# Attention in a hybrid decoder trunk: the transposed P moves from the three rotating score banks to the two banks of the value products

## The chip, the cores and the metric

The kernel runs on one core of one Trainium2 chip. The metric is the device time of one execution in microseconds, as the median of three runs. Engines are named as in the profile: PE (TensorE matmul), PEld (its weight loads), DVE (VectorE), ACT (ScalarE), POOL (GpSimd), SP (the queue that issues the DMAs). PSUM, into which PE writes, has eight banks of 128 partitions by 512 fp32 values. PE, ACT, DVE and POOL each work through a fixed list of instructions in order: an instruction that waits holds up all that stand behind it on the same engine.

## The reference

Two layers; each normalises x, multiplies it by one wide input matrix, runs two groups of heads side by side (a gated linear recurrence, HGRN2, and a sliding-window attention), gates both with SiLU, multiplies by an output matrix and adds the normalised result to x. SEQ is 512, D_MODEL 1024, and there are 16 attention heads of 64 in 2 key groups, with a window of 128. What matters here is the attention:

```
s = einsum('bnqkgd,bnskd->bnkgqs', qb, kw) * ATT_SCALE      # 128 queries x 256 keys per block
s = where(mask, s, NEG_INF)                                  # causal, at most 127 back
p = softmax(concatenate([s, sink], -1), -1)[..., :-1]        # one learned sink per head
o = einsum('bnkgqs,bnskd->bnqkgd', p, vw)
h_layer:  proj = h @ w_in;  y = concat(o_h, o_a) @ w_out;  x = x + rms_norm(y, g_post)
```

## The kernel before

**Projections.** All large products are done in three passes of split fp32 (`mm3`, L174 to L177): a value is held as a rounded part "hi" and a remainder "lo", and lo·hi, hi·lo and hi·hi are added in one PSUM bank. The weights come in pieces of 128x512 by DMA (`raw`); ACT rounds each to `whi` (L169), and DVE (for some POOL) subtracts it to get `wlo` (L170). The projection products write the three banks `pj`. They make up most of PE's work, and they are what fills PE while other stages wait for ACT, DVE and POOL.

**Banks.** Of the eight banks, three are `pj`, three rotate under `sc()` (each call takes the next of `sc0` to `sc2`, strictly in turn), and two are a pool under `ac()` (a call takes whichever is free):

```
sc_tiles = [ps.tile([P, 512], F32, tag=f"sc{i}", name=f"sc{i}", bufs=1) for i in range(SC)]
def sc():
    sc_turn[0] += 1
    return sc_tiles[sc_turn[0] % SC]
def ac():
    return ps.tile([P, 512], F32, tag="ac", name="ac", bufs=8 - PJ - SC)
```

**Attention.** Per layer there are 16 steps i = 4g + n, for four groups g of four heads and four blocks n of 128 queries. Each step has three parts, called here S, T and U:

- S(i), `att_scores`: the scores of four heads. For n = 0 they fill one bank (L417, eight matmuls of 128x128). For the other n they fill two banks, the halves S(i)a and S(i)b, of two heads each (L428, four matmuls of 128x256 per half). DVE masks them in place (L420, L432), takes the row maxima (L421, L433) and makes the bias `negm` (L436) and `ds` (L438); ACT takes the exponentials, one per head (L442, a READ_ACCUMULATOR row behind each), and `es` (L445); DVE adds and inverts the sums (L446, L447); POOL multiplies P by them (L449). The exponentials are the last readers of a score bank.
- T(i), `att_transpose`: PE transposes the four heads' P into one bank (L455); ACT rounds it (L267, out `a`), DVE takes the remainder (L268), and these two free the bank. POOL cuts out the two triangles `pcur` (or `b`) and `pprev` (L467).
- U(i), `att_value`: the value product in an `ac` bank (L481, four matmuls, two for n = 0). ACT copies one half out (`u`, L483), DVE adds the other to it in two instructions (`oa`, L487); the second of these frees the bank.

`att_stream` writes S(i), T(i-2), U(i-4) in turn, and `merge` weaves these 50 parts evenly into the projection steps that remain up to the first forget/query slab, FQ. A scheduler then fixes each engine's order: it keeps the written priority, but holds an instruction back while, by its own estimate, its bank or its inputs are not free. So who owns a bank decides where S, T and U stand among the projection matmuls. After the attention comes the recurrence (`hgrn`), which draws on both `sc` and `ac`. While the last attention steps run, ACT also works off FQ (L526 to L529: a load of its function table, two sigmoids, two scalings).

Of the kernel before, what the change touches and what calls it, by code (L numbers as in the profile page):

```python
# [65 lines left out]
def hybrid_kernel(ctx: ExitStack, tc: tile.TileContext, x, wkv, win, wout, g_pre, g_post, lbp, ghead, sinks,  # L66
# [12 lines left out]
    def pin(ins):  # L79
        return tc.keep_in_program_order(ins)  # L80
# [7 lines left out]
# [7 lines that stand above are left out]
    def tmp(tag, dt=F32, n=1):  # L95

        t = tp.tile([P, n, 512] if n > 1 else [P, 512], dt, tag=tag, name=tag, bufs=TB[tag])
        return t
# [167 lines left out]
    def split_psum(hi, lo, src):  # L266
        nc.scalar.copy(hi, src)  # L267
        nc.vector.tensor_tensor(lo, src, hi.bitcast(F32), op=ALU.subtract)  # L268
# [55 lines left out]
    def layer(l, last):  # L324
# [125 lines left out]
            return pt  # L450

        def att_transpose(g, n, pt, odd):
            T = sc()
            for h in range(4):
                pin(nc.tensor.transpose(T[:, h * P:(h + 1) * P], pt[:, h * P:(h + 1) * P], ident))  # L455
            tt_ = tmp("a", F32R, 2)
            split_psum(tt_[:, 0], tt_[:, 1], T)
            if n == 0:
                return [(n, tt_[:, 0]), (n, tt_[:, 1])]
            terms = []  # L460
            for which in range(2):
                if which == 0:
                    d = big.tile([P, 2, 512], F32R, tag="oy", name="pcur", bufs=6) if odd else tmp("b", F32R, 2)
                else:
                    d = big.tile([P, 2, 512], F32R, tag="q", name="pprev", bufs=QB)
                sg = -1 if which == 0 else 1
                nc.gpsimd.affine_select(out=d.rearrange("p a (h t) -> p (a h) t", h=4),  # L467
                                        in_=tt_.bitcast(F32).rearrange("p a (h t) -> p (a h) t", h=4),
                                        pattern=[[0, 8], [-sg, P]], compare_op=ALU.is_ge, fill=0.0,
                                        base=-which, channel_multiplier=sg)  # L470
                terms += [(n - which, d[:, 0]), (n - which, d[:, 1])]
            return terms
# [16 lines left out]
        def att_stream(steps):  # L489
            pts, terms = {}, {}  # L490
            n = len(steps)
            for tt in range(NT):
                ensure(("k", l, tt))
            for i in range(n + VLAG):
                if i < n:
                    until(lambda: steps[i][0] in qs)
                    pts[i] = att_scores(*steps[i])
                    yield 1.0
                if 2 <= i <= n + 1:
                    terms[i - 2] = att_transpose(*steps[i - 2], pts.pop(i - 2), i % 2)  # L500
                    yield 1.0
                if i >= VLAG:
                    att_value(*steps[i - VLAG], terms.pop(i - VLAG))
                    yield 1.0
# [181 lines left out]
        def zh_stream(s):  # L686
            def evac(tt, o):
# [9 lines left out]
                def rest():  # L697
                    T = sc()
                    for j in range(4):
                        pin(nc.tensor.transpose(T[:, j * P:(j + 1) * P], g[:, j * P:(j + 1) * P], ident))  # L700
                    Tv = T.rearrange("p (j t) -> p j t", j=4)
                    nc.scalar.activation(hi[:, :, t_], Tv, AF.Copy, scale=gh[:, l:l + 1])
                    nc.vector.scalar_tensor_tensor(lo[:, :, t_], Tv, gh[:, l:l + 1], hi[:, :, t_].bitcast(F32), op0=ALU.mult, op1=ALU.subtract)
# [153 lines left out]
def _tables():  # L857
# [3 lines left out]
    c, s = np.cos(ang).astype(np.float32), np.sin(ang).astype(np.float32)  # L861
    cf = np.ascontiguousarray(np.tile(c.T, (4, 1)))
    sf = np.ascontiguousarray(np.tile(s.T, (4, 1)))
# [47 lines left out]
```

## Time and profile before

| | |
|---|---|
| median of 3 runs | 956.77 us (952.09 to 960.68) |
| the profiled execution | 954.91 us, span 953.2 us, mean granted TensorE clock 0.989 |
| PE, PEld busy | 918.9 us (96%), 754.8 us (79%) |
| DVE, ACT, POOL busy | 681.9 us (72%), 475.2 us (50%), 267.3 us (28%) |
| attention on PE | about 80 to 188 us (layer 0) and 548 to 658 us (layer 1) |

The span runs from the first to the last instruction. Times in the traces count from its start. In a row of the timeline stand start, duration, engine, source line, what is written from what, and in brackets the idle time of the engine ahead of it with what ended it. Matmuls are pipelined, so that the duration of one (0.39 us) is longer than the distance to the next (0.23 us), which is what counts on PE. In a table of windows each row is a stretch of the span, with the busy time and the instructions of each engine, and the granted TensorE clock (PEclk, 1.00 is full).

### The profile page before, as it was taken

What the parts mean: (1) busy time and instruction counts of PE and PEld (TensorE: products, weight loads), DVE (VectorE), ACT (ScalarE), POOL (GpSimd) and SP (SyncE); (2) the same over time, 40 slices, a digit from 0 to 9 for tenths busy, and PEclk for the clock granted to TensorE, in tenths of its full rate; (3) what the DMA queues carried; (4) which work ended last, traced back from release to release, by engine and by line L of the source; (5) the groups of instructions that cost most, each with busy time, mean ns of one, the idle gap of its engine ahead of it and who ended that gap; (6) DMA issues with size and microseconds to landing.
All of it is one profiled execution on the core that took longest, in us unless ns stands there. A gap on an engine that the chain in (4) does not pass through costs nothing.

```text
span 953.2 us, 19110 instructions
## 1 busy us (share of the span) xinstructions
PE 918.9 (96%) x7228; PEld 754.8 (79%) x7228; DVE 681.9 (72%) x1382; ACT 475.2 (50%) x1135; POOL 267.3 (28%) x282
## 2 busy tenths in 40 slices
PE   7999998999999999999969989989999999999996
PEld 5887887778878788788868878877788887887885
DVE  5866878796766685865795678778867578749546
ACT  5524766836464462434553257677363645414242
POOL 2232454422231221311331235434322213113102
PEclk8999999999999999999999999999999999999999
DMA  6456622232222332323443665122222233413313
GB/s 219 145 177 175 186 72 79 66 90 68 78 79 81 87 112 89 112 69 118 132 158 123 178 180 150 54 70 67 90 67 69 88 89 84 129 55 103 89 46 132
DMA packets 56716, 101.34 MB, mean 106 GB/s; under 512 B 6448, under 2 KB 8880, under 8 KB 56624
## 3 DMA queue, kind: packets, MB, share of 16 engines
q1 hardware_dynamic: 56624, 100.12, 35.5%
q8 instruction: 57, 0.93, 0.4%
q14 instruction: 35, 0.29, 0.1%
HBM read 87.52 MB, written 12.58 MB: 105 GB/s over the span
## 4 chain that ended last, share of the span: by engine, by line
PE 77%; DVE 9%; ACT 6%; issue 4%; POOL 2%; DMA 1%; SPq 0%; DVEq 0%; POOLq 0%; ACTq 0%
PE pj L175 22%; PE pj L177 21%; PE pj L176 21%; DVE wlo L170 3%; ACT s L442 2%; PE sc L583 2%; PE sc L428 2%; PE ac L652 1%; PE ac L481 1%; PE ac L640 1%; ACT whi L169 1%; PE ac L655 1%; DVE xn L306 1%; PE sc L455 1%; PE sc L700 1%
## 5 line engine op out<-in xcount | busy, mean ns | idle before, releaser
L169 ACT CAST whi<-raw 128x512 fp32r<-128x512 f32 x256 | 158.2, 620 | 193.5 <-PE pj L177 154.3
L170 DVE TENSOR_TENSOR wlo<-raw,whi 128x512 fp32r<-128x512 f32 x248 | 185.4, 753 | 63.0 <-ACT whi L169 61.0
L175 PE MATMUL pj<-hhi,wlo 128*128 128x512 f32 x512 | 206.4, 403 | 0.0
L177 PE MATMUL pj<-hhi,whi 128*128 128x512 f32 x512 | 200.8, 392 | 0.0
L176 PE MATMUL pj<-hlo,whi 128*128 128x512 f32 x512 | 200.2, 391 | 0.0
L177 PEld LDWEIGHTS pj<-hhi,whi 128*128 128x128 f32 x512 | 96.6, 189 | 21.0
L175 PEld LDWEIGHTS pj<-hhi,wlo 128*128 128x128 f32 x512 | 96.6, 189 | 18.7
L176 PEld LDWEIGHTS pj<-hlo,whi 128*128 128x128 f32 x512 | 96.8, 189 | 18.2
L175 PE MATMUL pj<-whi,hlo 128*128 128x512 f32 x256 | 103.2, 405 | 3.6 <-ACT whi L169 3.6
L175 PE MATMUL pj<-whi,ops 128*128 128x512 f32 x256 | 103.8, 406 | 0.0
L176 PE MATMUL pj<-wlo,hhi 128*128 128x512 f32 x256 | 100.4, 392 | 0.0
L177 PE MATMUL pj<-whi,ops 128*128 128x512 f32 x256 | 100.1, 391 | 0.0
L177 PE MATMUL pj<-whi,hhi 128*128 128x512 f32 x256 | 100.1, 391 | 0.0
L176 PE MATMUL pj<-wlo,ops 128*128 128x512 f32 x256 | 99.7, 390 | 0.0
L601 POOL TENSOR_TENSOR k<-k,tot 128x256 f32<-128x256 f32 x80 | 65.0, 832 | 109.9 <-PE sc L583 64.0
L175 PEld LDWEIGHTS pj<-whi,hlo 128*128 128x128 f32 x256 | 48.2, 188 | 12.6 <-ACT whi L169 4.5
L449 POOL TENSOR_TENSOR s<-s,sums 128x512 f32<-128x512 f32 x32 | 34.9, 1091 | 81.9 <-DVE sums L447 34.3
L177 PEld LDWEIGHTS pj<-whi,ops 128*128 128x128 f32 x256 | 48.0, 188 | 10.7
L600 DVE TENSOR_TENSOR q<-q,tot 128x256 f32<-128x256 f32 x80 | 46.9, 614 | 13.1 <-PE sc L583 8.6
L177 PEld LDWEIGHTS pj<-whi,hhi 128*128 128x128 f32 x256 | 48.1, 188 | 10.1
L175 PEld LDWEIGHTS pj<-whi,ops 128*128 128x128 f32 x256 | 48.1, 188 | 9.3
L176 PEld LDWEIGHTS pj<-wlo,ops 128*128 128x128 f32 x256 | 48.2, 188 | 9.0
(172 smaller groups left out, 1587.0 us busy)
## 6 DMA issues: line engine op xcount, KB each, us to landing
raw<-in_win_dram SPq DMA_DIRECT2D x192, 256.0 KB, 2.7
raw<-in_wout_dram SPq DMA_DIRECT2D x64, 256.0 KB, 2.7
stack<-rot SPq DMA_DIRECT2D x16, 512.0 KB, 3.9
qs<-stack SPq DMA_DIRECT2D x32, 256.0 KB, 4.4
a<-in_x_dram SPq DMA_DIRECT2D x12, 256.0 KB, 3.1
raw<-in_wkv_dram SPq DMA_DIRECT2D x8, 256.0 KB, 4.0
x_mid<-a SPq DMA_DIRECT2D x8, 256.0 KB, 2.1
a<-x_mid SPq DMA_DIRECT2D x8, 256.0 KB, 3.2
```

Source lines behind the costliest of these rows:

```text
L169: nc.scalar.copy(hi, v)
L170: (nc.gpsimd if i in on_pool and i % 2 else nc.vector).tensor_tensor(lo, v, hi.bitcast(F32), op=ALU.subtract)
L175: nc.tensor.matmul(o, lhsT=sta[1], rhs=mov[0], start=start, stop=False)
L176: nc.tensor.matmul(o, lhsT=sta[0], rhs=mov[1], start=False, stop=False)
L177: nc.tensor.matmul(o, lhsT=sta[0], rhs=mov[0], start=False, stop=stop)
L306: nc.vector.scalar_tensor_tensor(xn, xt[c], r, g[c], op0=ALU.mult, op1=ALU.mult)
L428: pin(nc.tensor.matmul(S[:, h * 256:(h + 1) * 256], lhsT=q[:, 2 * hp_ + h, t_], rhs=kst[v][p][:, (n - 1) * P:(n + 1) * P], start=(h == 0 a ...
L442: nc.scalar.activation(pt[:, h * P:(h + 1) * P], cur[h], AF.Exp, bias=negm[:, h:h + 1], scale=SCALE, accum_out=sums[:, h:h + 1])
L449: nc.gpsimd.tensor_tensor(pv, pv, sums.unsqueeze(2).broadcast_to([P, 4, P]), op=ALU.mult)
L583: pin(nc.tensor.matmul(L[32 * b:32 * b + 32, c:c + 16], lhsT=k[:, o_:o_ + 32], rhs=qv[:, blk:blk + qu, 1, :], start=True, stop=True, tile_ ...
L600: nc.vector.tensor_tensor(qv[:, :, 1, :], qv[:, :, 1, :], tv[:, :, 0].unsqueeze(2).broadcast_to([P, nb, hh]), op=ALU.mult)
L601: nc.gpsimd.tensor_tensor(kv_[:, :, 0, :], kv_[:, :, 0, :], tv[:, :, 1].unsqueeze(2).broadcast_to([P, nb, hh]), op=ALU.mult)
```

## The change

T takes its bank from `ac()` instead of `sc()`. The scores have the three `sc` banks to themselves during the attention, and T and U share the two `ac` banks. Nothing is computed differently, and no instruction is added or removed.

```diff
         def att_transpose(g, n, pt, odd):
-            T = sc()
+            T = ac()
             for h in range(4):
                 pin(nc.tensor.transpose(T[:, h * P:(h + 1) * P], pt[:, h * P:(h + 1) * P], ident))
             tt_ = tmp("a", F32R, 2)
             split_psum(tt_[:, 0], tt_[:, 1], T)
```

What the change moves is the order on the engines. The places below are from layer 0; layer 1 has the same changes at nearly the same places. `sc_78` to `sc_80` are the three rotating score banks, x4 is a run of four equal rows.

PE at the head of the attention, from shortly behind S(1) to T(0). Before:

```order
L176 MATMUL pj<-wlo,hhi 128x512
L175 MATMUL pj<-whi,hlo 128x512
L177 MATMUL pj<-whi,hhi 128x512
L175 MATMUL pj<-whi,hlo 128x512 x2
L176 MATMUL pj<-wlo,hhi 128x512
L177 MATMUL pj<-whi,hhi 128x512
L428 MATMUL sc_79<-kst,qs 128x256 x4
L428 MATMUL sc_80<-kst,qs 128x256 x4
L175 MATMUL pj<-whi,hlo 128x512
L176 MATMUL pj<-wlo,hhi 128x512
L177 MATMUL pj<-whi,hhi 128x512
L455 MATMUL sc_78<-ident,s 128x128 x4
```

and now, the same stretch up to the two halves of S(2):

```order
L176 MATMUL pj<-wlo,hhi 128x512
L428 MATMUL sc_78<-kst,qs 128x256 x4
L177 MATMUL pj<-whi,hhi 128x512
L175 MATMUL pj<-whi,hlo 128x512
L176 MATMUL pj<-wlo,hhi 128x512
L177 MATMUL pj<-whi,hhi 128x512
L175 MATMUL pj<-whi,hlo 128x512 x2
L176 MATMUL pj<-wlo,hhi 128x512 x2
L177 MATMUL pj<-whi,hhi 128x512
L428 MATMUL sc_79<-kst,qs 128x256 x4
L428 MATMUL sc_80<-kst,qs 128x256 x4
```

A half of S(3), in sc_78, now stands ahead of S(2), 14 projection matmuls behind S(1); its bank was that of S(1)b. T(0) and T(1) then follow S(2) as one run of eight, and T(2) stands right behind S(4), ten projection matmuls earlier than before.

PE in the middle, around S(14), group 3, block 2. Before:

```order
L177 MATMUL pj<-hhi,whi 128x512
L175 MATMUL pj<-hhi,wlo 128x512
L428 MATMUL sc_79<-kst,qs 128x256 x4
L176 MATMUL pj<-hlo,whi 128x512
L428 MATMUL sc_80<-kst,qs 128x256 x4
L177 MATMUL pj<-hhi,whi 128x512
```

and now:

```order
L177 MATMUL pj<-hhi,whi 128x512
L428 MATMUL sc_79<-kst,qs 128x256 x4
L428 MATMUL sc_80<-kst,qs 128x256 x4
L175 MATMUL pj<-hhi,wlo 128x512
L176 MATMUL pj<-hlo,whi 128x512
L177 MATMUL pj<-hhi,whi 128x512
```

Before, S(13) stood in the same two banks as S(14); now S(13) stands in sc_80 and sc_78, so that only the second half of S(14) meets a bank of S(13). DVE's list from S(9) to `negm` of S(13) is the same in both but for the banks' names.

PE at the tail, from T(13) to U(11). Before there are six projection matmuls between the two:

```order
L455 MATMUL sc_78<-ident,s 128x128 x4
L175 MATMUL pj<-hhi,wlo 128x512
L176 MATMUL pj<-hlo,whi 128x512
L177 MATMUL pj<-hhi,whi 128x512
L175 MATMUL pj<-hhi,wlo 128x512
L176 MATMUL pj<-hlo,whi 128x512
L177 MATMUL pj<-hhi,whi 128x512
L481 MATMUL ac<-pcur,vst 128x512 x2
L481 MATMUL ac<-pprev,vst 128x512 x2
```

and now there are eleven (T(13) and the first of them are left out here):

```order
L176 MATMUL pj<-hlo,whi 128x512
L177 MATMUL pj<-hhi,whi 128x512
L175 MATMUL pj<-hhi,wlo 128x512
L176 MATMUL pj<-hlo,whi 128x512
L177 MATMUL pj<-hhi,whi 128x512
L175 MATMUL pj<-hhi,wlo 128x512
L176 MATMUL pj<-hlo,whi 128x512
L177 MATMUL pj<-hhi,whi 128x512
L175 MATMUL pj<-hhi,wlo 128x512
L176 MATMUL pj<-hlo,whi 128x512
L481 MATMUL ac<-pcur,vst 128x512 x2
L481 MATMUL ac<-pprev,vst 128x512 x2
```

U(11) stands five projection matmuls later. Behind it, counted from U(11), T(14) now stands 10 and U(12) 17 projection matmuls on (before 7 and 12), T(15) 23, U(13) and U(14) together 32, and U(15) 36 (before 18, 21, 47 and 50).

## The prediction

> **What bounds the kernel now.** I read the page first, then the waits of PE in each layer's attention, then windows around the places where PE stops, and last the timelines there.
>
> ```profile
> PE 918.9 (96%) x7228; PEld 754.8 (79%) x7228; DVE 681.9 (72%) x1382; ACT 475.2 (50%) x1135; POOL 267.3 (28%) x282
> ...
> PE 77%; DVE 9%; ACT 6%; issue 4%; POOL 2%; DMA 1%; SPq 0%; DVEq 0%; POOLq 0%; ACTq 0%
> ```
>
> PE is busy for 918.9 of the span's 953.2 us, and holds 77% of the chain that ended last: only PE's idle time can be won or lost. Next are PE's waits from 78 to 190 us (attention of layer 0; in total, times, longest), and the first two of the same list from 548 to 660 us (layer 1).
>
> ```profile
> PE sc L428 <- ACT s L442: 2.9, 2, 2.5
> PE pj L175 <- ACT whi L169: 1.4, 1, 1.4
> PE ac L481 <- DVE oa L487: 0.2, 1, 0.2
> PE sc L455 <- ACT es L445: 0.2, 1, 0.2
> PE sc L417 <- ACT s L442: 0.2, 1, 0.2
> PE sc L455 <- issue: 0.2, 1, 0.2
> PE sc L455 <- DVE negm L436: 0.2, 1, 0.2
> ```
>
> ```profile
> PE sc L428 <- ACT s L442: 2.9, 2, 2.6
> PE pj L175 <- ACT whi L169: 2.2, 1, 2.2
> ...
> ```
>
> Two waits are large: scores for exponentials (2.9 us in each layer, of which one is 2.5 or 2.6 and the other 0.4 or 0.3), and a projection product for a converted weight (1.4 and 2.2). The five short ones of layer 0 sum to 1.0 us; I take 0.9 per layer. The windows show what the large ones leave behind (the third number from the right is PEclk).
>
> ```profile
> 87.00:91.00 4.00, 2.59 (x13) 1.82 (x12) 2.30 (x8) 3.15 (x12) 2.60 (x2) 1.00 0.00 1
> 155.00:158.00 3.00, 1.08 (x5) 0.56 (x3) 2.97 (x6) 0.86 (x3) 1.75 (x2) 1.00 0.59 170
> 158.00:161.00 3.00, 2.37 (x10) 2.27 (x11) 2.54 (x7) 1.37 (x9) 0.77 (x1) 0.52 0.21 72
> 161.00:164.00 3.00, 3.00 (x16) 2.48 (x16) 1.74 (x6) 1.18 (x5) 1.04 (x1) 0.91 0.00 0
> 556.00:560.00 4.00, 1.78 (x8) 1.18 (x7) 1.93 (x6) 3.76 (x17) 2.25 (x2) 1.00 0.00 0
> 628.00:631.00 3.00, 2.93 (x13) 2.60 (x14) 2.89 (x10) 0.81 (x6) 1.07 (x2) 0.69 0.17 61
> 631.00:634.00 3.00, 3.00 (x13) 2.44 (x13) 1.04 (x3) 1.63 (x8) 0.17 (x1) 0.74 0.01 3
> 700.00:800.00 100.00, 100.00 (x1065) 82.17 (x1064) 70.52 (x131) 48.13 (x94) 23.18 (x29) 1.00 0.27 80
> ```
>
> In the recurrence (700 to 800) PE has no gap, and by the order of the instructions none of its matmuls there changes its place. So the whole effect must come from the two attention stages. There PE stops at the head of each layer (87 to 91, 556 to 560) and in the middle (155 to 158 in layer 0, ahead of 628 in layer 1). Behind the middle stop the clock falls: it costs 3 x (0.48 + 0.09) = 1.7 us in layer 0 and 3 x (0.31 + 0.26) = 1.7 us in layer 1. At the head it stays at 1.00.
>
> **The middle stop.** Rows of PE, POOL, DVE and ACT in order of time, layer 0.
>
> ```profile
> 155.47 0.39 PE L177 MATMUL pj<-hhi,whi 128*128 128x512 f32 x1
> 155.70 0.39 PE L175 MATMUL pj<-hhi,wlo 128*128 128x512 f32 x1
> ...
> 156.25 1.48 POOL L467 TENSOR_SCALAR_AFFINE_SELECT pcur<-a 128x1024 fp32r<-128x1024 f32 x1 [3.15 <-DVE a L268]
> 156.70 1.04 DVE L436 SCALAR_TENSOR_TENSOR negm<-mx,nsnk 128x4 f32<-128x4 f32 x1
> ...
> 158.38 0.20 ACT L442 ACTIVATION_READ_ACCUMULATOR s<-sc,negm 128x1 f32 x1
> ...
> 158.63 1.22 PE L428 MATMUL sc<-kst,qs 128*128 128x256 f32 x4 [2.55 <-ACT s L442]
> ```
>
> S(14)a, at 158.63, waited 2.55 us for a bank of S(13), until the second exponential of S(13) was read at 158.58. Those exponentials waited for `negm`, which took 1.04 us on DVE beside POOL's `pcur`. Is the bank the cause? Only in part. Now S(14)a has a free bank, but S(14)b stands right behind it in the bank of S(13)a, and needs the same two exponentials. DVE's list up to that `negm` is unchanged and the T and U ahead keep their places, so the exponentials end when they did. PE does half a score during the stop, in place of one projection matmul: 0.48 us (S(1), quoted below: eight matmuls in 1.12 us less a tail of 0.16, halved) less 0.23 (155.70 - 155.47), at half clock twice that. **-0.5 us per layer.** The stop shrinks from 2.55 to about 2.3 us. I take the clock to fall as before; if it does not, 1.7 us per layer go too.
>
> The other wait of L428 is S(13)b for S(12), 0.37 us. S(12) and S(13) now stand in three different banks: **-0.4 us per layer**. The short waits all stand at places that change: **-0.9**, and what is new is counted below.
>
> [...]
>
> **The head.** Here the change costs. The scheduler sees a free bank earlier, and puts half of S(3) 14 projection matmuls behind S(1), in the bank of S(1)b.
>
> ```profile
> 82.24 1.12 PE L428 MATMUL sc<-kst,qs 128*128 128x256 f32 x8
> ...
> 88.47 0.21 ACT L442 ACTIVATION_READ_ACCUMULATOR s<-sc,negm 128x1 f32 x1
> ...
> 89.34 0.50 PE L175 MATMUL pj<-whi,hlo 128*128 128x512 f32 x1 [1.41 <-ACT whi L169]
> ...
> 96.50 1.04 POOL L449 TENSOR_TENSOR s<-s,sums 128x512 f32<-128x512 f32 x1 [5.59 <-DVE sums L447]
> ...
> 557.89 0.23 ACT L442 ACTIVATION_READ_ACCUMULATOR s<-sc,negm 128x1 f32 x1
> ...
> 558.77 0.50 PE L175 MATMUL pj<-whi,hlo 128*128 128x512 f32 x1 [2.22 <-ACT whi L169]
> ```
>
> S(1) gives way to the projections at 83.20; 14 matmuls of 0.23 us later it is 86.4. The bank is free when the fourth exponential of S(1) has been read, at 88.68. So PE stops there for 2.2 us ahead of work that it could do: before, it issued six more projection matmuls and then waited 1.41 us for `whi`. At 89.3 it is six matmuls (1.4 us) behind and half a score (0.5) ahead, and `whi` is there by then. Layer 0: **+0.9 us**. In layer 1 the half stands 17 matmuls behind S(1), three ahead of the old stop; it is released at 558.1 and ends at 558.6, while the old stop ended at 558.77: 0.7 - 0.5 - 0.1 = **+0.1 us**.
>
> T(2) comes ten matmuls earlier, right behind S(4). Before, POOL's product for step 2 ended at 97.54. S(2) came six matmuls behind 89.34 and ended at 91.9, so that the way from S(2) to T(2) takes 5.6 us. Now 12 projection matmuls, T(0), T(1), half a score and S(4) lie between: 2.8 + 0.9 + 0.5 + 1.0 = 5.2 us (a T is about half of S(1)'s eight matmuls). It is 0.4 us too early, and 1.4 if the maxima of S(3)a and the cast of T(1), which stand ahead of step 2 now, add their 0.4 and 0.6: 0 to 1.4 us; I take 0.8, since both stand there in the order. **+0.8 us per layer.**
>
> **The tail.** T and U now pass through two banks: U(11) waits for the bank of U(10), T(14) for that of T(13), U(12) for that of U(11). Rows of PE, ACT and DVE, layer 0:
>
> ```profile
> 169.72 0.62 PE L481 MATMUL ac<-pcur,vst 128*128 128x512 f32 x2
> 169.76 0.58 ACT L483 COPY u<-ac 64x512 f32<-64x512 f32 x1
> ...
> 170.38 0.85 DVE L487 TENSOR_TENSOR oa<-ac,u 64x256 f32<-64x256 f32 x2 [1.54 <-ACT u L483]
> ...
> 173.14 0.60 ACT L267 CAST a<-sc 128x512 fp32r<-128x512 f32 x1
> ...
> 173.77 0.69 DVE L268 TENSOR_TENSOR a<-sc,a 128x512 fp32r<-128x512 f32 x1
> 174.38 1.05 DVE L170 TENSOR_TENSOR wlo<-raw,whi 128x512 fp32r<-128x512 f32 x1
> ...
> 175.69 1.24 DVE L170 TENSOR_TENSOR wlo<-raw,whi 128x512 fp32r<-128x512 f32 x1
> ```
>
> U(10)'s bank is free at 171.23, when both `oa` are done; its copy stood on ACT behind FQ until 169.76. U(11) was issued at 169.72; five matmuls later is 170.9: a wait of 0.4 us. T(14) needs the remainder of T(13), done at 174.46; PE is there at 171.3 + 0.9 + 10 x 0.23 = 174.5: none. U(12) needs the two `oa` of U(11). U(11)'s copy stands on ACT behind the cast of 173.14 and two weight casts and ends near 175.5; DVE has the remainder and two `wlo` ahead until 176.7 (174.38, 175.69; both beside POOL), and 0.85 us of `oa` make 177.6. PE comes at 174.5 + 0.4 + 7 x 0.23 = 176.5: a wait of 1.1 us. T(15), U(13), U(14) and U(15) have 4 to 15 matmuls of room each, and by the same count find their banks free. **+1.5 us per layer**; from nothing, with `wlo` at its undisturbed 0.69 us (that of L268) and ACT early, to 3, with one more 1.24 us ahead of U(12) or U(13). In the steady steps T and U have most of a step to empty a bank, and wait for nothing.
>
> Also moved: in layer 1, SP issues a store of rotated queries ahead of a weight piece that had to wait for its buffer. The store goes earlier, the piece does not: nothing.
>
> **Sum.** Layer 0: -0.5 - 0.4 - 0.9 + 0.9 + 0.8 + 1.5 = +1.4; layer 1: +0.6 (the head 0.8 less). Together **+2.0 us**. On the profiled execution (954.91, which is 1.86 us under the median) this is 956.9, on the median of 956.77 it is 958.8; I give 957.8, between them. The waits move from bank to bank; the chain of DVE, ACT and POOL in a step is as long as it was.
>
> **Rivals.**
> 1. *The score waits go.* DVE gets its masks earlier, `negm` slips ahead of POOL's `pcur`, and both middle stops vanish with the cold clock: 2.55 + 2.6 + 3.4 = 8.5 us in place of the 1.0 counted: 957.8 - 7.5 = 950.3 us. If the new waits of T(2) and the tail were nil as well (1.6 + 3.0), 945.7. For it: this is the largest wait on the list. Against: S(14)b meets a bank of S(13), and DVE's list is the same.
> 2. *The two shared banks become the bound at the tail.* A U waits for the copy of the U before, which stands on ACT behind FQ's table load and four activations; T waits for U, and U for T. From a wait of about 2.5 us on, the clock falls as at 158: per layer 3.0 in place of 1.5, and 1.7 cold, 6.4 us in all; with the same drop behind both stops at the head another 3.4: 964 to 968 us. For it: U(10) was copied 5 us after its matmuls. Against: my count leaves waits near 1 us. [...]
> 3. *The shortened middle stops no longer drop the clock* (2.3 us, near the 2.22 that did not): 957.8 - 3.4 = 954.4 us.
>
> **How the numbers follow.** Forecast 0.62, rival 1 0.12, rival 2 0.12, rival 3 0.14. The unknown costs give from 957.8 - 1.6 - 3.0 - 3.4 = 949.8 (new waits nil, clock up) to 964 (rival 2 without the head); I let go of the outermost and take 951 to 964. About 1%, 9.6 us, is what a measurement of this kernel can tell from no change. Faster by that needs rival 1 with nothing new waiting: 0.05. Slower needs rival 2 at its upper end: 0.08. Within: 0.87.
>
> **What would show it.** In the profile after: in layer 0, L428 waiting for L442 about 2.2 us near 86.5; no wait ahead of S(13)b; S(14)b still waiting near 158, a stop of some 2.3 us with a clock near 0.5 behind it; a wait of T(2) for POOL; waits of L481 for DVE `oa` near U(11) and U(12), 1.5 us per layer; the recurrence as it was. I am wrong if the middle stop is gone, or if any tail wait exceeds 2 us.

## The result and the profile after

The change made the kernel slower: 965.43 us in the median of 9 runs (963.35 to 966.25) against 956.78 us for the kernel before (952.09 to 960.68), a ratio of 1.008 with a 95% interval of 1.006 to 1.010. That is 8.7 us where 2.0 had been forecast, and outside the range. The profiled execution took 966.25 us, the longest of the nine, so that it shows rather more than the median loses.

The page of the kernel after, its busy times and its chain:

```profile
PE 920.6 (95%) x7228; PEld 758.1 (79%) x7228; DVE 691.5 (72%) x1382; ACT 474.3 (49%) x1135; POOL 269.3 (28%) x282
...
PE 70%; DVE 13%; ACT 8%; issue 5%; POOL 3%; DMA 2%; SPq 0%; DVEq 0%; POOLq 0%; ACTq 0%
```

PE's busy time is nearly the same. What has grown is the part of the chain that is not PE: DVE went from 9% to 13%, ACT from 6% to 8%, DMA from 1% to 2%. The place is the attention, as forecast. From the start of S(0) (79.95 before, 80.76 after) to the first matmul of the recurrence (199.60 and 206.03) layer 0 took 119.7 us before and 125.3 after; layer 1 took 120.6 and 125.5. Between the two stages lie 349.0 and 349.1 us.

PE's waits after, 78 to 190 us and 548 to 670 us (in total, times, longest):

```profile
PE sc L428 <- ACT s L442: 5.0, 2, 2.9
PE ac L481 <- DVE oa L487: 2.0, 3, 0.9
PE ac L455 <- POOL s L449: 1.3, 1, 1.3
PE ac L455 <- DVE a L268: 1.3, 1, 1.3
```

```profile
PE sc L428 <- ACT s L442: 5.1, 2, 2.8
PE ac L481 <- DVE oa L487: 2.4, 4, 0.9
PE ac L455 <- POOL s L449: 1.6, 1, 1.6
PE ac L455 <- DVE a L268: 1.3, 1, 1.3
```

The same waits in their places, PE's timeline of layer 0, in order S(3)a, T(2), U(4), T(7), U(9), S(14)b, U(12), U(15):

```profile
89.53 0.79 PE L428 MATMUL sc<-kst,qs 128*128 128x256 f32 x4 [2.15 <-ACT s L442]
...
101.35 0.66 PE L455 MATMUL ac<-ident,s 128*128 128x128 f32 x4 [1.33 <-POOL s L449]
...
127.16 0.70 PE L481 MATMUL ac<-a,vst 128*128 128x512 f32 x2 [0.29 <-DVE oa L487]
...
132.82 0.63 PE L455 MATMUL ac<-ident,s 128*128 128x128 f32 x4 [1.27 <-DVE a L268]
...
158.88 0.70 PE L481 MATMUL ac<-pcur,vst 128*128 128x512 f32 x2 [0.82 <-DVE oa L487]
...
164.74 0.89 PE L428 MATMUL sc<-kst,qs 128*128 128x256 f32 x4 [2.86 <-ACT s L442]
...
183.31 0.69 PE L481 MATMUL ac<-a,vst 128*128 128x512 f32 x2 [0.90 <-DVE oa L487]
...
191.08 0.70 PE L481 MATMUL ac<-pcur,vst 128*128 128x512 f32 x2 [0.47 <-DVE oa L487]
```

Behind the stops at the head the clock fell this time (windows, third number from the right):

```profile
88.00:92.00 4.00, 2.48 (x9) 2.09 (x10) 2.06 (x7) 3.11 (x12) 2.08 (x2) 0.76 0.00 0
92.00:96.00 4.00, 4.00 (x23) 3.40 (x22) 2.46 (x7) 0.40 (x1) 0.00 (x0) 0.82 0.71 250
564.00:568.00 4.00, 3.33 (x10) 2.85 (x11) 2.41 (x6) 2.25 (x8) 1.87 (x2) 0.57 0.03 6
```

That is 4 x (0.24 + 0.18) = 1.7 us in each layer of this execution. Over the nine executions the mean granted clock was 0.982 to 0.989, so the clock did not cost the same in all of them.

Three waits were not forecast at all: U(4), T(7) and U(9), 2.4 us together. T(7) waits for a remainder on DVE. The chain of the kernel after, 118 to 128 us (start, us, what; rows of `issue` are left out), says where DVE was:

```profile
118.83 0.70 DVE wlo L170
...
119.55 4.28 DMA raw<-in_win_dram
...
123.85 0.63 ACT whi L169
...
124.51 0.69 DVE wlo L170
125.20 0.97 DVE negm L436
...
126.20 1.50 ACT s L442 x8
```

The chain goes through a **transfer of a weight piece**. `negm` of S(7) stands on DVE behind the `wlo` of that piece, and the piece had not landed. It was late because of the head. Rows of DVE and SP after, and behind them the same two and `negm` of S(7) before:

```profile
105.73 1.46 DVE L170 TENSOR_TENSOR wlo<-raw,whi 128x512 fp32r<-128x512 f32 x1
...
107.22 0.35 SPq L152 DMA_DIRECT2D raw<-in_win_dram  x1
```

```profile
99.79 0.69 DVE L170 TENSOR_TENSOR wlo<-raw,whi 128x512 fp32r<-128x512 f32 x1 [0.44 <-ACT whi L169]
...
100.51 0.35 SPq L152 DMA_DIRECT2D raw<-in_win_dram  x1
...
119.29 0.14 DVE L436 SCALAR_TENSOR_TENSOR negm<-mx,nsnk 128x4 f32<-128x4 f32 x1
```

Counted from S(0), the first `wlo` behind the masks of S(2) came after 19.8 us before and after 25.0 us now, and with it the refill of its buffer, 5.9 us later (20.6 and 26.5): a `raw` buffer, of which there are three, is filled again only when its `wlo` is done. From that first `wlo` to `negm` of S(7) DVE has eight pieces in both kernels. That `negm` ended 39.5 us after S(0) before and 45.4 us after it now, again 5.9 us later. The exponentials of S(7) and S(8) follow from it, and behind them on ACT stands the cast of T(6) (131.36), whose remainder T(7) waits for.

The transfer in this chain was also slow by itself: 4.28 us from issue to landing, where the one issued 1.2 us ahead of it took 2.61. Four loads of `qs` (256 KB each) were issued 0.4 to 1.9 us behind it. Before, the piece in the same place in SP's order had 1.6 us to the first of these loads and took 2.68 us. That the loads slow it is likely by these rows, but no run tests it.

### The profile page after: what moved, and what is told of

Read it like the earlier page. It is cut to its first block, busy times and chain, and to the rows that moved or that the text cites. A ratio compares the mean times of both kernels' runs of the same rounds, so it can differ in the third digit from the quotient of the medians.

```text
span 964.5 us, 19096 instructions
## 1 busy us (share of the span) xinstructions
PE 920.6 (95%) x7228; PEld 758.1 (79%) x7228; DVE 691.5 (72%) x1382; ACT 474.3 (49%) x1135; POOL 269.3 (28%) x282
## 4 chain that ended last, share of the span: by engine, by line
PE 70%; DVE 13%; ACT 8%; issue 5%; POOL 3%; DMA 2%; SPq 0%; DVEq 0%; POOLq 0%; ACTq 0%
PE pj L175 21%; PE pj L177 20%; PE pj L176 19%; DVE wlo L170 3%; ACT s L442 3%; PE sc L583 2%; PE ac L652 1%; PE ac L640 1%; DVE oa L487 1%; PE ac L655 1%; ACT whi L169 1%; DVE mx L433 1%; DVE a L268 1%; DVE xn L306 1%; DVE negm L436 1%
## 5 line engine op out<-in xcount | busy, mean ns | idle before, releaser
L442 ACT ACTIVATE s<-sc,negm 128x128 f32<-128x128 f32 x128 | 45.5, 368 | 43.2 <-DVE negm L436 43.1
L177 PEld LDWEIGHTS pj<-whi,hhi 128*128 128x128 f32 x256 | 48.7, 190 | 10.5
L176 PEld LDWEIGHTS pj<-wlo,hhi 128*128 128x128 f32 x256 | 48.9, 191 | 8.3
```

Source lines behind the costliest of these rows:

```text
L176: nc.tensor.matmul(o, lhsT=sta[0], rhs=mov[1], start=False, stop=False)
L177: nc.tensor.matmul(o, lhsT=sta[0], rhs=mov[0], start=False, stop=stop)
L442: nc.scalar.activation(pt[:, h * P:(h + 1) * P], cur[h], AF.Exp, bias=negm[:, h:h + 1], scale=SCALE, accum_out=sums[:, h:h + 1])
```

## The experiments

All were timed in 3 or 5 rounds beside the kernel before. The head means T(0) to T(2) and what the scheduler puts around them; the tail means T(13) on.

| kernel | median, us | ratio to before (95%) |
|---|---|---|
| the change | 965.4 | 1.008 (1.006 to 1.010) |
| T(0) to T(2) in `ac` alone | 968.5 | 1.013 (1.011 to 1.016) |
| T(3) to T(15) in `ac` alone | 956.7 | 1.001 (0.999 to 1.003) |
| T(13) to T(15) in `ac` alone | 960.4 | 1.003 (1.001 to 1.005) |
| all T in `ac`, S in the banks of before | 968.4 | 1.013 (1.010 to 1.015) |
| T(0) in `ac` alone | 963.4 | 1.006 (1.004 to 1.008) |
| T(2) to T(15) in `ac` | 959.3 | 1.002 (1.001 to 1.004) |
| the change, one turn skipped at T(0) | 962.2 | 1.005 (1.003 to 1.007) |
| four `raw` buffers, before | 954.2 | 0.997 (0.996 to 0.999) |
| four `raw` buffers, the change | 958.2 | 1.001 (1.000 to 1.003) |
| four `raw` buffers, the change, tail in `sc` | 958.0 | 1.001 (1.000 to 1.003) |
| `negm` early, before | 958.8 | 1.002 (1.001 to 1.004) |
| four `raw` buffers and `negm` early, before | 955.1 | 0.998 (0.997 to 1.000) |
| `negm` early, T(0) to T(2) in `ac` | 958.0 | 1.000 (0.998 to 1.002) |
| `negm` early, the change | 958.1 | 1.002 (1.000 to 1.003) |

### Which part of the attention costs

The line of the change was made to depend on the step:

```diff
-            T = ac()
+            T = ac() if 4 * g + n < 3 else sc()
```

> T(0), T(1) and T(2) alone take an `ac` bank, T(3) to T(15) an `sc` bank as before. By the order of the instructions half of S(3) again stands 14 projection matmuls behind S(1), and everything from S(6) on stands as in the kernel before. Theory A (the head costs: a stop of 2.2 us with a clock that falls behind it, and an early T(2)): L428 waits 2.2 us near 89 us, the clock in 88 to 92 is near 0.76, T(2) waits 1.3 us; that is +0.75 + 1.7 + 1.3 = 3.8 us in layer 0 and 0.1 + 1.7 + 1.6 = 3.4 us in layer 1, so about 964 us where the kernel before has 956.8. Theory B (T and U sharing two banks costs, in the steady steps and at the tail; the head is made up for by later slack): 957 to 958 us.

```diff
-            T = ac()
+            T = sc() if 4 * g + n < 3 else ac()
```

> The converse: T(0) to T(2) take an `sc` bank as before, T(3) to T(15) an `ac` bank as in the change, so that the head is as before and the middle and the tail are as changed. Theory A: the waits of T(7), U(4), U(9) and of the tail sum to at most 3.7 us per layer against 0.9 to 1.3 us of short waits and the wait of S(13)b that go: 960 to 962 us. Theory B: the time of the change less little, 964 to 965 us. If the whole loss is the cold clock at the head: 957 to 958 us.

```diff
-            T = ac()
+            T = ac() if 4 * g + n >= 13 else sc()
```

> T(13), T(14) and T(15) alone take an `ac` bank; the head and the steady steps are as before, and the tail stands as in the change or a little later. By the tail's rows in the change (U(12) 0.9 us, U(15) 0.4 to 0.5 us) it costs 1.4 us per layer: 959 to 960 us under both theories. 962 us or more would mean that the tail costs more than its waits show; 956 to 957 us that its waits are made up for behind it.

The three bank choices of the head alone gave 968.5 us, more than the whole change; all the others without them gave 956.7. So the loss lies at the head, as theory A has it, but it is larger than A's 7 us. The tail alone cost 3.5 us where about 3 had been expected, but that is luck: in its trace no U of the tail waits for `oa`, and the only new wait there is U(15) for POOL's `pcur` and `pprev`, 0.9 us in each layer. Nor do the parts add: the tail costs 3.5 us alone, and nothing where T(3) to T(12) are in `ac` too. PE's waits with T(3) to T(15) in `ac`, 78 to 190 us:

```profile
PE sc L428 <- ACT s L442: 2.9, 1, 2.9
PE ac L481 <- DVE oa L487: 2.1, 3, 0.9
PE pj L175 <- ACT whi L169: 1.4, 1, 1.4
```

U(9), U(12) and U(15) still wait (2.1 us together), but T(7) does not, though T and U share the two banks from T(3) on and stand from S(7) on as in the change. The sharing alone therefore does not make T(7) wait; the head has to be there too. With the head alone it has become a larger one. Its rows of PE, ACT and DVE:

```profile
123.43 0.62 ACT L169 CAST whi<-raw 128x512 fp32r<-128x512 f32 x1 [2.47 <-DMA raw<-in_win_dram]
124.08 0.69 DVE L170 TENSOR_TENSOR wlo<-raw,whi 128x512 fp32r<-128x512 f32 x1 [2.40 <-ACT whi L169]
124.69 0.16 DVE L436 SCALAR_TENSOR_TENSOR negm<-mx,nsnk 128x4 f32<-128x4 f32 x1
125.74 1.68 PE L417 MATMUL sc<-kst,qs 128*128 128x128 f32 x8 [3.44 <-ACT s L442]
```

S(8) stops for 3.44 us here (3.47 in layer 1), because its bank is one of S(7) again, whose exponentials wait for the late `negm`. Behind the stop in layer 0 PE's projection matmuls stood 0.43 us apart in place of 0.23, until about 129.6. In the change the scores have three banks to themselves, S(8) finds a free one, and T(7) waits 1.27 us: the rest of the change seems to soften what its head does.

### Which part of the head costs

```diff
+            sc()
             T = ac()
```

> T takes an `ac` bank as in the change, but one turn of the score banks is skipped at each T, so that every S stands in the bank in which it stood before: T and U share two banks and the scores gain nothing. By the order no half of S(3) stands early. Theory B (the sharing costs): T(7), U(4), U(9), U(12) and U(15) wait as in the change, 3.7 us per layer, and the middle stop of S(14) is that of before: about +5 to +7 us, 962 to 964 us. Theory A (the head costs, through the freed score banks): the clock at the head stays at 1.00, and the time is 957 to 960 us.

This missed: 968.4 us without an early half of S(3). T(7) did not wait, nor did U(4) or U(9), so theory B, which had the time too low as well, is not borne out. PE's stops were 0.48 us at T(2), 1.58 at the second half of S(5), 1.14 at T(4) and 1.29 at a half of S(9): T stands as early as `ac` allows, ahead of POOL's product, and the scores stop for banks that are not free. An early half of S(3) is thus not needed for a loss of this size; but here T and U share two banks in every step while the scores gain none, so this run alone does not say which of the two costs.

```diff
-            T = ac()
+            T = ac() if 4 * g + n == 0 else sc()
```

> T(0) alone takes an `ac` bank. By the order half of S(3) stands early, in the bank of S(1)b, as in the change, but T(1) and T(2) stand 15 and 10 projection matmuls apart behind T(0) and S(3) (350 and 360 counted from the start of the stage's list, before 345 and 354, in the change 335 and 344). Theory A1 (the early half itself costs: PE stops 2.2 us, the clock falls, and S(2) and all weight work on DVE behind it come 2 us later, which returns as later stops): 962 to 966 us. Theory A2 (T(1) and T(2), put too early, cost): only the stop and the clock are left, about 2.4 us in layer 0 and 1.8 us in layer 1: 960 to 961 us at most, and 957 to 958 us if that is made up for behind it.

```diff
-            T = ac()
+            T = sc() if 4 * g + n < 2 else ac()
```

> T(0) and T(1) take an `sc` bank as before, T(2) and all later ones an `ac` bank; the kernel with T(0) to T(2) in `sc` banks gave 956.7 us. By the order T(2) and U(0) stand five projection matmuls earlier than before, ahead of S(4) and S(5), and no half of S(3) stands early. Theory A1 (only the early half costs): 956 to 958 us. Theory A2 (an early T is enough): T(2) waits 1 to 1.5 us for POOL's product, the steps behind it come late, 960 to 966 us.

```diff
+            if 4 * g + n == 0: sc()
             T = ac()
```

> As the change, with one turn of the score banks skipped ahead of T(0): S(3) stands in the banks in which it stood before. By the order its first two matmuls stand 22 projection matmuls behind S(1) and no longer 14, where their bank is about free, and T(0), T(1) and T(2) stand as early as in the change (336 and 342). Theory A1: the stop at the head is under 0.5 us, the clock stays at 1.00, and the time is 957 to 960 us. Theory A2: T(2) waits 1.3 us or more, and 962 to 967 us.

Both theories hold in part. The early half with late T's cost 6.1 us, and the early T's almost without an early half 4.9 us (the two early matmuls of that kernel are rows of L417, so they belong to S(4) and not to S(3)). The two together (T(0) to T(2) in `ac`) cost 11.6. T(2), put five projection matmuls earlier, cost 2.0 us, between the ranges of the two theories, with waits of 0.4 us at T(2) and 0.45 at T(4). In layer 0 ACT waited for weight pieces 0, 1.4 and 1.8 us with T(0) alone, with the turn skipped and with T(2) on, and 3.2 us in the change; in layer 1 0.6, 2.7 and 0, and 2.7 in the change. In none of the three did T(7) or S(8) stop for more than 0.2 us. So it took both parts of the head to make that stop. Late pieces do not explain the 6.1 us of T(0) alone: beside the stops at the head its trace has a new one of 1.57 us in each layer, ahead of a half of S(5) whose bank was not free.

### The sharing by itself

A fourth buffer for weight pieces gives both kernels nearly the same head:

```diff
-RAW_BUFS = 3
+RAW_BUFS = 4
...
-                st = sm.tile([P, 3, P], F32, tag="st", name="st", bufs=2)
+                st = sm.tile([P, 3, P], F32, tag="st", name="st", bufs=1)
```

> The kernel before with four buffers for weight pieces instead of three (the space comes from the recurrence's state tile `st`, one buffer instead of two). By the order S(2) stands 18 projection matmuls earlier and T(0) 17 earlier. It is the base for the next kernel; the time itself is open, 948 to 966 us: the wait for `whi` at the head (1.4 and 2.2 us) should shrink, and the recurrence may slow.

> The same four buffers with the change. By the order the heads of the two kernels are alike now: S(2) at 315 and 318 and T(0) at 321 in both, T(1) at 333 (334 without the change), T(2) at 342 in both, and no half of S(3) early. Theory A (the change costs at the head, by what the scheduler puts there early): within 1.5 us of the kernel without the change. Theory B (T and U in two banks cost in the steady steps and at the tail): 5 to 7 us slower than it.

> As the kernel with four buffers and the change, but T(13), T(14) and T(15) take an `sc` bank again. The kernel with the change and four buffers gave 958.2 us, the one without the change 954.2 us. If the difference of 4 us is the tail (U(11) 0.9, U(12) 0.9, U(15) 0.5 us, 2.3 us in each layer): these waits go, and the time is 953 to 955 us. If it comes from the steady steps: 957 to 959 us.

With like heads the change costs 4.0 us, half of what it costs with three buffers: more than theory A allowed (1.5) and less than theory B asked for (5 to 7). PE's waits for `oa` (78 to 190 us) with the change, and below them those with the tail put back:

```profile
PE ac L481 <- DVE oa L487: 2.5, 4, 0.9
```

```profile
PE ac L481 <- DVE oa L487: 1.0, 1, 1.0
PE sc L455 <- issue: 1.0, 1, 1.0
```

Putting the tail back took away 1.5 us of U's waits and brought 1.0 us at a T, and the time did not move (958.0). By the traces the 4 us are waits of PE: in the two attention stages they sum to 12.0 us with four buffers, 16.0 with the change as well, and 15.4 with the tail put back. The time of the last had been expected for a loss in the steady steps, but both its wait for `oa` and that at a T stand at the tail. The waits there change places when the banks do, and why they stay was not settled. Nor is the price a fixed one: with three buffers T(3) to T(15) in `ac` cost nothing. Four buffers without the change gave 954.2 us (0.996 to 0.999 of the time before): this version beats both kernels, by little.

### The middle stop

```diff
+                with tc.high_priority(200):
                     nc.vector.copy_predicated(...)   # L420, L432
                     nc.vector.tensor_reduce(...)     # L421, L433
...
+            with tc.high_priority(200):
                 negm = ...; ds_ = ...                # L435 to L438
```

> The kernel before with a higher priority for the masks, the maxima, `negm` and `ds` on DVE. By the order `negm` of S(13) stands ahead of a `wlo` and of a remainder (L268) behind which it stood before, 1.3 to 1.9 us earlier; the head and the tail keep their places within one to four matmuls. If the middle stop hangs on that `negm`: the stop of 2.55 us shrinks to 0.7 to 1.3 us in both layers and the clock stays at 1.00 behind it, 950 to 953 us. If it hangs on the banks or on ACT's other work: 956 to 958 us.

> Four buffers for the weight pieces, no change of T's bank, and the higher priority for the masks, the maxima, `negm` and `ds`. The buffers alone gave 954.2 us; the priority alone took away the middle stop of 2.55 us and its cold clock, and got 1.7 and 1.0 us of new stops at the tail, 958.8 us. If the two add: the stops at the head of 1.1 and 0.5 us that came with the priority stay away here, 951 to 954 us. If the tail's stops give back all that the middle gains: 954 to 957 us.

The middle stop hung on `negm`, as the prediction said: it is gone in both layers, and in layer 0 PE's projection matmuls there stand 0.23 us apart. And yet the time is 958.8 us, no better than before. PE's waits with the priority, 78 to 190 us, first three of the list:

```profile
PE sc L429 <- ACT s L445: 2.1, 3, 1.1
PE sc L458 <- issue: 1.7, 1, 1.7
PE pj L175 <- ACT whi L169: 1.4, 1, 1.4
```

PE now waits at the tail: 1.7 us ahead of T(14), while ACT works off FQ and two table loads of 1.28 us ahead of the exponentials, and 1.0 us ahead of U(13) for `oa`, which stands on DVE behind two `wlo` of 3.07 us together. In the steps behind the head 1.1 and 0.5 us of new stops came with the order. One reading is that the score stops are a symptom of how long a step takes on DVE and ACT; the runs do not show more than that one stop went and others came. With four buffers as well it is 955.1 us, which is no gain over the buffers alone (954.2): the two do not add.

### Is it the late weight piece?

The priority has another use. With the head unchanged it moves `negm` of S(7) ahead of the `wlo` that was late, and of one more. DVE's list with T(0) to T(2) in `ac`, from the last mask of S(7) on (L435 stands for L433, L439 for L436), without and with the priority:

```
L433 mx    L170 wlo x2   L433 mx     L268 a     L170 wlo (late)   L436 negm
L435 mx    L435 mx       L170 wlo    L439 negm  L170 wlo          L441 ds   L490 oa   L170 wlo (late)
```

> T(0) to T(2) in `ac` banks, the others in `sc`, with the higher priority for the masks, the maxima, `negm` and `ds`. The head stands as in the kernel with T(0) to T(2) in `ac` alone (968.5 us), but `negm` of S(7) now stands ahead of the `wlo` that waited there for a late weight piece (2.40 us for ACT's cast, which waited 2.47 us for the DMA). Theory D (the early head makes a weight piece late, and the piece holds up `negm` of S(7) on DVE): the stop of S(8), 3.44 and 3.47 us, shrinks to under 1.5 us, and the middle stop goes as it did with the priority alone; 960 to 963 us. Theory E (the delay runs from step to step over T, U and the banks, the piece is by the way): S(8) still stops for 2.5 us or more; 964 to 968 us.

> The change with the same priority. `negm` of S(7) again stands ahead of the late `wlo`. Theory D: T(7), which waited 1.27 and 1.26 us for a remainder on DVE, waits under 0.6 us, and the stops at the head (2.2 us, T(2) 1.3 us) stay: 961 to 964 us. Theory E: T(7) waits as before or S(8) takes its place, 964 to 967 us.

With T(0) to T(2) in `ac` the time fell from 968.5 to 958.0 us, below what theory D had named. Rows of DVE, ACT and PE, layer 0 (L439 is `negm`):

```profile
121.41 0.15 DVE L439 SCALAR_TENSOR_TENSOR negm<-mx,nsnk 128x4 f32<-128x4 f32 x1
123.94 0.62 ACT L169 CAST whi<-raw 128x512 fp32r<-128x512 f32 x1 [1.14 <-DMA raw<-in_win_dram]
124.97 1.11 PE L417 MATMUL sc<-kst,qs 128*128 128x128 f32 x8 [1.62 <-ACT s L445]
```

The pieces are as late as before (ACT waits 3.0 us for them in layer 0, 4.3 without the priority), and so are the stops at the head (2.16 and 1.32 us). But `negm` no longer stands behind the last piece: S(8)'s stop falls from 3.44 to 1.62 us (theory D had said under 1.5), with the cast at 123.94 still between two exponentials, and in layer 1 from 3.47 to nothing. That is 5.3 us of stops and, at 1.7 us a fall, 1.7 us of slow clock behind layer 0's (3.4 us if layer 1's had one behind it too): most of the 10.5 us. The middle stops went as well, 2.54 us in each layer, but 1.70 and 1.0 us came at the tail in their place. That bears theory D out for this kernel.

For the change itself T(7)'s wait went too, and so did the middle stop; U(3) now waits 1.23 and 0.68 us for `oa`, and U(11) 2.33 us in both layers. How much of its 7.3 us of gain is the late piece cannot be read from this run.

Taken together: with `negm` behind the weight pieces the head costs 11.6 us and the change 8.7; with `negm` ahead of them the head gives 958.0, the change 958.1 and the kernel before 958.8 us. The visible stops at the head stay in both kernels, and cost nothing there. So what made the head cost lies in what it did to DVE's list. With T(0) to T(2) in `ac` it is `negm` behind late weight pieces; in the change this is argued from its chain and from the totals, because the priority moves the masks and maxima of every step along with `negm`.

## Why the prediction was wrong, step by step

- **The head, 0.9 and 0.1 us.** The stop itself came out as forecast (2.2 and 2.15 us), but not its price: this is the step that failed. With T(2) the head was put at 2.6 us for both layers; alone it cost 11.6 us, and the change without it cost nothing. The step counted PE's matmuls and took "`whi` is there by then". That held for the next product, which did not wait. But the step never followed the casts and remainders that the early S and T push back on ACT and DVE: the first `wlo` behind S(2) came 5.1 us later, and `negm` of S(7) 5.9 us. The part on the order showed DVE's list from S(9) to S(13); the change was in DVE's list from S(2) to S(7).
- **"In the steady steps T and U have most of a step to empty a bank, and wait for nothing"** failed: U(4), T(7) and U(9) waited 2.4 us in layer 0. U(9) waits from the sharing (0.7 us without the head); T(7) and U(4) do not wait without the head.
- **"At the head it stays at 1.00"** was the clock of one execution. Behind the change's stops it fell, 1.7 us in each layer; behind stops of one length it fell in one kernel's profile and stayed in another's (below).
- **T(2)**, 0.8 us: 1.33 and 1.60. The upper bound of 1.4 was the better reading in layer 0.
- **The middle**: S(13)b's wait went, the short waits went, S(14)b still stopped and the clock fell, as said. The stop was 2.86 us and not 2.3; the saving of 0.5 us for the half score did not show.
- **The tail**, 1.5 us: U(12) and U(15) 1.4 us in both layers. The size was right, U(11) found its bank free, and U(15) waited in its place.
- **The recurrence** as it was: right.
- **The signs of being wrong**, a middle stop that is gone or a tail wait over 2 us: neither came, and the time was off all the same. They watched the middle and the tail, and not the steps behind the head.

Layer 0 adds up so: stop at the head 2.15 in place of 1.41, +0.7; clock +1.7; T(2) +1.3; U(4), T(7), U(9) +2.4; middle -0.1; tail +1.4; short waits -0.9: 6.5 us, where the stage shows 5.6. The difference of 0.9 us is PE's matmuls and its gaps under 0.15 us, which took that much less (112.7 us before, 111.8 after, at full clock); why was not taken apart. So in this execution T(7)'s wait, the one that hangs on the late piece, is 1.3 us of the layer, and the clock at the head 1.7.

Of the rivals, the first (the score waits go) was priced at 7.5 us of gain; the kernel with the priority fulfilled its condition (both middle stops and their slow clock gone), and gained nothing. The second named a time of 964 to 968 us, where the change came to lie, but for another reason: its tail waits of 2.5 us did not come, and only its stops at the head did. The 2.5 us from which it let the clock fall was read off one trace, and so was the 2.2 us behind which the third let it stay: in the runs the clock fell behind a stop of 2.15 us and stayed behind one of 2.85.

## What to carry to other kernels

Where a scheduler fixes the order by its own estimates, a bank that comes free is also a permission to put work earlier, and in-order engines then stand in front of it, PE here for 2.15 us. Compare the order on every engine from the first place that moves, and look for what is pushed back there, the loads of the next inputs above all: with few buffers a late cast becomes a late transfer a few steps on (here, with three, 5.9 us later). A stop that vanishes is worth nothing until it is known which wait is late next.

## What the runs showed of the hardware

Behind some stops of PE the granted clock fell to 0.50, behind others it stayed at 1.00. The six falls in the attention of the kernel before and of the change lasted 3.41 us each, which loses 1.7 us (0.50 of 3.41). With T(2) to T(15) in `ac`, and with one turn skipped at T(0), it took PE longer: its projection matmuls, 0.23 us apart at full clock, stood 0.43 us apart, as they do in the change at a clock of 0.50, from 161.13 to 166.2 and from 164.58 to 169.6.

Layer 0 of both kernels and of twelve others, and layer 1 of both, have 47 stops of PE over 1.1 us; in the twelve a fall is read from these distances. Behind none of the 23 of 1.13 to 1.71 us did the clock fall; it did behind 12 of the 23 of 2.02 to 2.88 us, and behind the one of 3.44 us. Stops of one length go either way. Behind the 2.15 us ahead of S(3)a it fell in the change, and stayed with T(0) to T(2) in `ac` alone and with T(0) alone. Behind a middle stop of 2.85 us it fell with T(2) to T(15) in `ac`, and stayed with four buffers and the change. And behind layer 1's stop at the head it stayed before (2.22 us) and fell with the priority:

```profile
561.00:564.00 3.00, 3.00 (x19) 2.35 (x17) 2.85 (x8) 1.88 (x7) 0.00 (x0) 1.00 1.00 272
```

```profile
561.00:564.00 3.00, 3.00 (x13) 2.68 (x12) 2.58 (x6) 0.00 (x0) 0.21 (x1) 0.51 0.84 267
```

The fall is not tied to the end of the stop either: in the change it came at 90.07, 0.54 us behind the stop's end at 89.53; before, at 158.11, 0.52 us ahead of the end at 158.63. What decides was not shown. So one profile does not tell whether a stop of 2 to 3 us is followed by a slow clock, and a forecast has to give it a chance: by these counts, as an estimate, about a half at 2.02 to 2.88 us, at a price of 1.7 us.
